# The first norm's shift and scale vectors: sixteen tiles with the weights as the stationary operand, instead of four on VectorE and twelve as rows

## The chip, the core and the metric

The kernel runs on one core of a Trainium2 chip. The metric is the device time of one execution in microseconds (us). TensorE is called PE in the profile, its weight loads PEld, VectorE DVE, ScalarE ACT, GpSimd POOL and the queue that issues the DMAs SP.

## The reference, cut to what matters

The program is two layers of a transformer-like trunk over 640 tokens (512 latent, 128 context) of width 1024. A layer normalises its input with a shift and a scale that come from a conditioning vector, projects it, runs three token mixers, merges them, and ends in a normalised MLP:

```python
mod = jax.nn.silu(cond) @ lp['w_mod'] + lp['b_mod']
sh1, sc1, gt1, sh2, sc2, gt2 = jnp.split(mod, 6, axis=-1)
h = rms_norm(x, lp['g_norm1']) * (1 + sc1) + sh1
... = jnp.split(h @ lp['w_in'], offsets, axis=-1)
```

There are two conditioning vectors, one for latent and one for context tokens. sh1 and sc1 of layer 0 are 2048 columns of w_mod, 8.4 MB in float32, and no projection can start without them. All the rest of w_mod (the other 80 tiles of 128 columns) is needed later.

## The kernel before, in words

Activations lie with channels on the partitions: x is eight tiles of 128 channels by 640 tokens, worked in two halves of 256 and 384 tokens. The large projections split each operand into a rounded part and a rest, so that each block takes three matmuls (L104 to L106, or the same three lines with operands exchanged); load_w loads a weight tile, rounds it on ACT (L97) and takes the rest on DVE or, in the first projections, on POOL (L99).

Nothing orders the work by hand. The program is written as one stream; a planner that is part of the framework puts each engine's instructions, and the issues on the SP queue, into an order by priority (program order) and by when it reckons them ready. On the chip each engine then works strictly in that order, and an instruction that waits holds up all behind it. SP also waits where a buffer has to be released.

Before the first projection (run, L1350 to L1375) the kernel does this:

- mod_first (three calls): 512 shift or scale columns at a time. The conditioning, two columns wide, is the stationary operand and the weights stream through, 512 columns per matmul (L223); float32 matmuls leave two records each. The two rows that come out are copied (L225), transposed (L228) and finished on DVE. Its weights come in 1 MB pieces into two buffers, mraw.
- cond_rows: 16 matmuls (L198) and four ACT copies spread the conditioning over all partitions, in condb.
- mod_tile (four calls at the start): the other 512 columns as dot products on DVE against condb (L209), weights in four 512 KB tiles, sraw.
- stat_add: squares of x on ACT (L262, L266), summed on DVE (L267). norm_scale: column sums by matmuls against a vector of ones (L285), the inverse root on DVE (L126 to L133, twelve small instructions for each half), and its spread over partitions by matmuls (L289).
- norm_apply: per channel tile and token part, nt (DVE, L300), hh (ACT, L303) and hl (DVE, L304).
- consts2 and tables load masks (two buffers, cast on DVE, L175), rope tables and a row; then mla_down starts three projections: proj_tail, and proj_nat twice. Its first two outputs (proj_tail, 48 matmul records 192 columns wide) come first, then proj_nat, 256 wide.

Later, at the start of layer 0's merge, cond_rows runs once more, and 80 further mod_tile calls are strewn over merge, out_proj and mlp, with one buffer, modw.

Of the kernel before, what the change touches and what calls it, by code (L numbers as in the profile page):

```python
# [11 lines left out]
F32 = mybir.dt.float32  # L12
# [4 lines left out]
ALU = mybir.AluOpType  # L17
# [4 lines left out]
D = 1024  # L22
# [46 lines left out]
    "xin": ("xin", 3), "mjunk": ("mj", 1), "condb": ("mj", 1), "modw": ("mj", 1), "mraw": ("st", 2), "sraw": ("st", 4), "maskf": ("st", 2), "mrow": ("st", 2), "uh": ("mlp", 8), "ul": ("mlp", 8), "relu": ("mlp", 3),  # L69
# [5 lines left out]
class Net:  # L75
# [125 lines left out]

    def mod_tile(self, l, i, buf="modw"):

        nc = self.nc
        w = self.S([128, 1024], F32, buf)
        nc.sync.dma_start(w, self.a["wmod"][l, i])
        for s in range(2):
            junk = self.S([128, 1024], mybir.dt.bfloat16, "mjunk")
            nc.vector.tensor_tensor_reduce(  # L209
                out=junk, in0=w, in1=self.condb[:, s], scale=1.0, scalar=0.0,  # L210
# [4 lines left out]
    def mod_first(self, b, kind):  # L215

        nc = self.nc
        p = self.P([128, 512], "g")
        for j in range(2):
            w = self.S([128, 4, 512], F32, "mraw")  # L220
            nc.sync.dma_start(w, self.a["wmods"][kind, b, j])
            for k in range(4):
                nc.tensor.matmul(p[0:2], self.csil[:, j * 4 + k::8], w[:, k], start=(j + k == 0), stop=(j + k == 4))  # L223
        row = self.S([2, 512], F32, "mrow")
        nc.scalar.copy(row, p[0:2])  # L225
        p = self.P([128, 4, 2], "g")
        for i in range(4):
            nc.tensor.transpose(p[:, i], row[:, i * 128:i * 128 + 128], self.ident[0:2, 0:2])  # L228
        i0 = kind * 8 + b * 4
        nc.vector.tensor_copy(self.modv[0][:, i0:i0 + 4], p)  # L230
        self.mod_fin(0, i0, 4)
# [26 lines left out]
    def stat_add(self, x, half):  # L258
# [8 lines left out]
        nc.vector.tensor_tensor(self.sq[:, c0:c1], self.sq[:, c0:c1], t[:, :c1 - c0], op=ALU.add)  # L267
# [1362 lines left out]
```

## Time and profile before

| what | value |
|---|---|
| median of three runs | 2676.58 us (2673.47 to 2679.17) |
| profiled execution, its own time | 2678.4 us |
| its span, first to last instruction | 2676.6 us |
| mean granted TensorE clock | 0.978 of full |
| TensorE matmul busy | 2538.1 us, 95% of the span |
| VectorE, ScalarE, GpSimd busy | 60%, 45%, 16% |

Busy time is the union of an engine's instructions; a pipelined matmul's record lasts longer than the step from one to the next, so rates are read from the start times. A clock of 1.00 is 2.4 GHz and 0.50 is 1.2 GHz. An arrow in square brackets says for how long the engine was idle before and what released it.

### The profile page before, as it was taken

The numbers are of one execution on the slowest core, as the hardware profiler recorded it, in microseconds if no ns is written. First come the engines' busy times: TensorE is split into PE (matmuls) and PEld (weight loads), VectorE is DVE, ScalarE is ACT, GpSimd is POOL, SyncE is SP. The second block draws the span as 40 slices with busy tenths as digits, with TensorE's granted clock in tenths as the row PEclk, the third lists the DMA queues.
The fourth block names the chain that finished last, engine by engine and source line by source line (L and its number), as shares of the span: only waits on it lengthen the run. The fifth ranks groups of instructions, "written<-read, shape, count | busy, mean of one in ns | idle before, by whom it ended". The sixth has DMA issues, their size and how long they took to land.

```text
span 2676.6 us, 45051 instructions
## 1 busy us (share of the span) xinstructions
PE 2538.1 (95%) x17596; PEld 2446.5 (91%) x17596; DVE 1596.4 (60%) x3635; ACT 1192.4 (45%) x2323; POOL 432.9 (16%) x582
## 2 busy tenths in 40 slices
PE   6999999799898999999989998998989999999999
PEld 3988899788898999999989888987879999999999
DVE  6488664676866776666365776647855346333332
ACT  4476775465222342232335776756642335132230
POOL 2021131310222021020121222213002101010110
PEclk8999999899999999999999999998999999999999
DMA  6111111312745444444221112122134242222221
GB/s 250 40 46 68 57 56 40 98 54 70 257 147 167 165 142 150 150 150 135 87 78 52 47 57 71 41 74 72 49 118 156 74 141 75 79 72 78 73 78 48
DMA packets 105268, 258.47 MB, mean 97 GB/s; under 512 B 11808, under 2 KB 43296, under 8 KB 104288
## 3 DMA queue, kind: packets, MB, share of 16 engines
q1 hardware_dynamic: 105056, 255.59, 28.5%
q8 instruction: 139, 2.28, 0.3%
q14 instruction: 73, 0.60, 0.1%
HBM read 229.43 MB, written 26.12 MB: 95 GB/s over the span
## 4 chain that ended last, share of the span: by engine, by line
PE 72%; DVE 12%; ACT 7%; DMA 4%; issue 3%; POOL 1%; SPq 0%; DVEq 0%; ACTq 0%; POOLq 0%
PE g L105 18%; PE g L104 18%; PE g L106 18%; DMA modw<-wmod 2%; PE f L104 2%; PE f L106 2%; PE f L105 2%; DVE mjunk L209 2%; PE go L498 2%; PE y L1018 1%; PE g L814 1%; DVE wlo L99 1%; PE g L1010 1%; DVE sm_m L746 1%; ACT whi L97 1%
## 5 line engine op out<-in xcount | busy, mean ns | idle before, releaser
L97 ACT CAST whi<-wraw 128x1024 fp32r<-128x1024 f32 (+2 forms) x236 | 220.1, 932 | 440.2 <-PE g L105 373.8
L99 DVE TENSOR_TENSOR wlo<-wraw,whi 128x1024 fp32r<-128x1024 f32 (+3 forms) x230 | 258.9, 1127 | 225.7 <-ACT whi L97 220.0
L106 PE MATMUL g<-hh,wlo 128*128 128x256 f32 (+1 forms) x1072 | 332.2, 310 | 4.2 <-DVE wlo L99 4.2
L104 PE MATMUL g<-hh,whi 128*128 128x256 f32 (+1 forms) x1072 | 332.0, 310 | 3.2 <-ACT gth L1179 2.7
L105 PE MATMUL g<-hl,whi 128*128 128x256 f32 (+1 forms) x1072 | 331.6, 309 | 0.0
L1292 POOL TENSOR_TENSOR relu<-relu 128x256 f32<-128x256 f32 (+1 forms) x128 | 110.6, 865 | 805.2 <-ACT uh L1291 795.3
L209 DVE CUSTOM_DVE_ANT_0 mjunk<-modw,condb 128x1024 bf16<-128x1024 f32 x160 | 199.5, 1247 | 68.5 <-DMA modw<-wmod 65.6
L97 ACT CAST xhi<-xraw 128x1024 fp32r<-128x1024 f32 (+1 forms) x80 | 83.7, 1046 | 283.6 <-PE g L105 264.2
L106 PEld LDWEIGHTS g<-hh,wlo 128*128 128x128 f32 x1072 | 203.2, 190 | 5.4 <-DVE wlo L99 5.4
L104 PEld LDWEIGHTS g<-hh,whi 128*128 128x128 f32 x1072 | 202.9, 189 | 4.8 <-ACT gth L1179 3.3
L105 PEld LDWEIGHTS g<-hl,whi 128*128 128x128 f32 x1072 | 203.3, 190 | 0.0
L1241 DVE SCALAR_TENSOR_TENSOR x<-g,moda,x 128x256 f32<-128x256 f32 (+1 forms) x192 | 78.4, 435 | 200.6 <-PE g L106 200.6
L104 PE MATMUL g<-hh,xhi 128*128 128x384 f32 (+1 forms) x544 | 168.1, 309 | 0.0
L106 PE MATMUL g<-hh,xlo 128*128 128x384 f32 (+1 forms) x544 | 168.0, 309 | 0.0
L105 PE MATMUL g<-hl,xhi 128*128 128x384 f32 (+1 forms) x544 | 167.8, 308 | 0.0
L104 PE MATMUL g<-uh,xhi 128*128 128x384 f32 (+1 forms) x512 | 158.2, 309 | 0.0
L106 PE MATMUL g<-uh,xlo 128*128 128x384 f32 (+1 forms) x512 | 158.0, 309 | 0.0
L105 PE MATMUL g<-ul,xhi 128*128 128x384 f32 (+1 forms) x512 | 158.0, 309 | 0.0
L106 PE MATMUL g<-uh,wlo 128*128 128x384 f32 (+1 forms) x512 | 158.0, 309 | 0.0
L105 PE MATMUL g<-ul,whi 128*128 128x384 f32 (+1 forms) x512 | 157.9, 308 | 0.0
L104 PE MATMUL g<-uh,whi 128*128 128x384 f32 (+1 forms) x512 | 157.9, 308 | 0.0
L1228 POOL TENSOR_TENSOR x<-x,th 128x256 f32<-128x256 f32 x64 | 75.7, 1188 | 496.8 <-DVE th L1226 496.6
(445 smaller groups left out, 7664.1 us busy)
## 6 DMA issues: line engine op xcount, KB each, us to landing
modw<-wmod SPq DMA_DIRECT2D x80, 512.0 KB, 3.5
wraw<-w SPq DMA_DIRECT2D x64, 512.0 KB, 3.5
xraw<-w SPq DMA_DIRECT2D x64, 512.0 KB, 3.5
wraw<-wfm SPq DMA_DIRECT2D x62, 512.0 KB, 3.5
wraw<-wn SPq DMA_DIRECT2D x36, 512.0 KB, 3.6
wraw<-wo SPq DMA_DIRECT2D x48, 256.0 KB, 3.2
yin<-yd SPq DMA_DIRECT2D x24, 320.0 KB, 3.9
mraw<-wmods SPq DMA_DIRECT2D x6, 1024.0 KB, 6.1
```

Source lines behind the costliest of these rows:

```text
L97: nc.scalar.copy(hi, raw)
L99: eng.tensor_tensor(lo, raw, hi.bitcast(F32), op=ALU.subtract)
L104: mm(out, wh, xh, start=first, stop=False)
L105: mm(out, wh, xl, start=False, stop=False)
L106: mm(out, wl, xh, start=False, stop=last)
L209: nc.vector.tensor_tensor_reduce(out=junk, in0=w, in1=self.condb[:, s], scale=1.0, scalar=0.0, op0=ALU.mult, op1=ALU.add, accum_out=self.m ...
L498: nc.tensor.matmul(p[:, hd], km[:, hd, cs], qm[:, hd, cs])
L746: nc.vector.tensor_reduce(out=nm, in_=sc, axis=ax, op=ALU.max, negate=True)
L814: nc.tensor.transpose(p[:, i * 256 + j * 128:i * 256 + j * 128 + 128], pts[j][:, (k0 + i) * 128:(k0 + i) * 128 + 128], self.ident)
L1228: nc.gpsimd.tensor_tensor(mg[m][:, c0:c1], mg[m][:, c0:c1], t[:, c0:c1], op=ALU.add)
L1241: self.nc.vector.scalar_tensor_tensor(dst[:, p0:p1], p[:, p0 - c0:p1 - c0], self.moda[l][:, kind * 8 + m, s:s + 1], src[:, p0 - o:p1 - o], ...
L1292: nc.gpsimd.tensor_tensor(r[:, :n], r[:, :n], r[:, :n], op=ALU.mult)
```

## The change

The sixteen tiles of 128 columns (eight of shift, eight of scale) are all computed by PE with the roles exchanged: the weight block of 128 by 128 is the stationary operand, the two columns of conditioning stream through, eight matmuls a tile. The result lies on the partitions already, so that one ACT instruction per tile adds the bias (and, for the scale, multiplies by the gain) and no row is copied or transposed. Weight tiles of 512 KB use twelve buffers: two are loaded ahead of x, ten behind it, four as buffers come free. The order is scale and shift of channel tile 0, then of tile 1, and so on, with norm_apply following tile by tile. The inverse norm is computed once for all five blocks of 128 tokens. The sum of squares of the second half goes to POOL. The first cond_rows call and the four mod_tile calls are gone; the remaining cond_rows, at the merge, loads the two conditioning rows by a DMA that broadcasts them to all partitions and applies the silu there, with half of it left to the dot product's scale. The weights' host layout changes with it.

```diff
     "xin": ("xin", 3), "mjunk": ("mj", 1), "condb": ("mj", 1), "modw": ("mj", 1), 
-    "mraw": ("st", 2), "sraw": ("st", 4), "maskf": ("st", 2), "mrow": ("st", 2), ...
+    "mraw": ("st", 12), "maskf": ("st", 2), ...
     def cond_rows(self):
         cb = self.S([128, 2, 1024], F32, "condb")
+        nc.sync.dma_start(cb, self.a["condr"].to_broadcast([128, 2, 1024]))
         for s in range(2):
-            for q in range(2):
-                p = self.P([128, 512], "g")
-                for j in range(4):
-                    c = self.csil[:, s * 8 + q * 4 + j:][:, 0:1]
-                    nc.tensor.matmul(p[:, j * 128:j * 128 + 128], c.to_broadcast([128, 128]), self.ident)
-                nc.scalar.copy(cb[:, s, q * 512:q * 512 + 512], p)
+            th = self.S([128, 1024], F32, "modw")
+            nc.scalar.activation(th, cb[:, s], AF.Tanh, scale=0.5)
+            nc.vector.scalar_tensor_tensor(cb[:, s], th, 1.0, cb[:, s], op0=ALU.add, op1=ALU.mult)
...
-    def mod_first(self, b, kind):
+    def mod_load(self, j):
+        w = self.S([128, 8, 128], F32, "mraw")
+        self.nc.sync.dma_start(w, self.a["wmods"][j])
+        return w
+    def mod_first(self, k, kind, w):
         p = self.P([128, 512], "g")
-        for j in range(2):
-            w = self.S([128, 4, 512], F32, "mraw")
-            nc.sync.dma_start(w, self.a["wmods"][kind, b, j])
-            for k in range(4):
-                nc.tensor.matmul(p[0:2], self.csil[:, j * 4 + k::8], w[:, k], start=(j + k == 0), stop=(j + k == 4))
-        row = self.S([2, 512], F32, "mrow")
-        nc.scalar.copy(row, p[0:2])
...
+        for j in range(8):
+            nc.tensor.matmul(p[:, 0:2], w[:, j], self.csil[:, j::8], start=(j == 0), stop=(j == 7))
+        i = kind * 8 + k
+        if kind == 0:
+            nc.scalar.activation(self.moda[0][:, i], p[:, 0:2], AF.Identity, bias=self.bmod[:, 0, i:i + 1])
+        else:
+            nc.scalar.activation(
+                self.moda[0][:, i], p[:, 0:2], AF.Identity, bias=self.bg[:, k:k + 1], scale=self.vec[:, 0, k:k + 1])
...
-        nc.vector.tensor_tensor(self.sq[:, c0:c1], self.sq[:, c0:c1], t[:, :c1 - c0], op=ALU.add)
+        (eng or nc.vector).tensor_tensor(self.sq[:, c0:c1], self.sq[:, c0:c1], t[:, :c1 - c0], op=ALU.add)
...
+    def norm_scale_all(self):
+        bc = [self.P([128, 512], "n") for half in range(2)]
+        st = bc[0][:, 384:389]
+        for i in range(5):
+            nc.tensor.matmul(st[:, i:i + 1], self.sq[:, i * 128:i * 128 + 128], self.one)
+        r = self.S([128, 5], F32, "nr5")
+        self.rsqrt(r, st, 1.0 / D, 5)
+        for i in range(5):
+            half, j = (0, i) if i < 2 else (1, i - 2)
+            nc.tensor.matmul(bc[half][:, j * 128:j * 128 + 128], r[:, i:i + 1].to_broadcast([128, 128]), self.ident)
...
-            self.mod_first(0, 1)
+            order = [(k, kind) for k in range(8) for kind in (1, 0)]
+            ws = {j: self.mod_load(j) for j in range(2)}
             for k in range(8):
                 nc.sync.dma_start(xs[k], a["x"][:, k])
                 for i in range(2):
-                    self.stat_add(xs[k], i)
-            self.cond_rows()
-            for i in range(4):
-                self.mod_tile(0, i, "sraw")
+                    self.stat_add(xs[k], i, nc.gpsimd if i else nc.vector)
             self.norm_begin()
-            for half in range(2):
-                self.norm_scale(half)
-            self.mod_first(1, 1)
-            self.mod_first(1, 0)
-            for k in (0, 4):
-                for half in range(2):
-                    self.norm_apply(0, 0, xs, half, range(k, k + 4))
+            for j in range(2, 12):
+                ws[j] = self.mod_load(j)
+            for j in range(2):
+                self.mod_first(*order[j], ws.pop(j))
+            self.norm_scale_all()
+            for k in range(8):
+                for j in (2 * k, 2 * k + 1):
+                    if j > 1:
+                        self.mod_first(*order[j], ws.pop(j))
+                    if j + 10 < 16 and j + 10 > 11:
+                        ws[j + 10] = self.mod_load(j + 10)
+                self.norm_apply(0, 0, xs, 0, (k,))
+                if k < 6:
+                    self.norm_apply(0, 0, xs, 1, (k,))
+            self.norm_apply(0, 0, xs, 1, (6, 7))
             self.consts2()
```

## Rows read from the trace of the kernel before

**Rows 1.** The page, part 1: busy us (share of the span) and instructions of each engine

```profile
PE 2538.1 (95%) x17596; PEld 2446.5 (91%) x17596; DVE 1596.4 (60%) x3635; ACT 1192.4 (45%) x2323; POOL 432.9 (16%) x582
```

**Rows 2.** Windows of 10 us: PE, PEld, DVE, ACT, POOL busy; clock, DMA share, GB/s

```profile
10.00:20.00 10.00, 9.33 (x42) 4.07 (x41) 6.12 (x16) 7.58 (x19) 0.00 (x0) 1.00 1.04 417
...
60.00:70.00 10.00, 10.00 (x65) 10.00 (x65) 6.82 (x19) 4.33 (x12) 4.67 (x13) 0.73 0.17 57
...
100.00:110.00 10.00, 10.00 (x75) 10.00 (x75) 6.81 (x39) 5.10 (x19) 0.00 (x0) 1.00 0.13 37
```

**Rows 3.** Timeline of the start: start us, us, engine, line, operation, tiles, forms

```profile
7.80 8.51 PE L223 MATMUL g<-mraw,csil 128*2 128x512 f32 x16 [7.80 <-DMA mraw<-wmods]
...
20.99 1.17 PE L285 MATMUL n<-one,sqacc 128*128 128x1 f32 x10
...
21.68 0.15 DVE L126 TENSOR_SCALAR rq_v<-n 128x2 f32<-128x2 f32 x1
...
32.12 2.50 PE L289 MATMUL n<-ident,nr 128*128 128x128 f32 x10 [5.05 <-DVE nr L133]
...
52.97 0.36 PE L104 MATMUL g<-whi,hh 128*128 128x192 f32 x1
...
57.85 0.53 PE L106 MATMUL g<-xhi,hl 128*128 128x192 f32 x1 [1.49 <-DVE hl L304]
...
65.27 0.40 PE L104 MATMUL g<-whi,hh 128*128 128x256 f32 x1
```

**Rows 4.** Timeline of the SP queue at the start

```profile
2.58 0.91 SPq L221 DMA_DIRECT2D mraw<-wmods  x2
...
19.02 0.33 SPq L311 DMA_DIRECT2D rowb<-row  x1
32.53 0.80 SPq L174 DMA_DIRECT2D maskf<-mask  x2
...
46.18 0.33 SPq L174 DMA_DIRECT2D maskf<-mask  x1
```

**Rows 5.** Short windows with the granted clock (last three columns as in Rows 2)

```profile
38.00:38.50 0.50, 0.50 (x3) 0.09 (x2) 0.31 (x1) 0.50 (x3) 0.50 (x1) 0.87 0.00 0
...
60.00:64.00 4.00, 4.00 (x21) 4.00 (x20) 4.00 (x8) 2.25 (x5) 2.37 (x1) 0.50 0.03 12
...
65.00:65.50 0.50, 0.50 (x4) 0.50 (x4) 0.50 (x3) 0.50 (x2) 0.00 (x0) 0.56 0.98 401
...
1382.00:1386.00 4.00, 3.09 (x13) 2.85 (x13) 2.10 (x12) 0.00 (x0) 0.00 (x0) 0.50 0.38 131
```

**Rows 6.** Timeline of PE at layer 1's first norm

```profile
1382.36 1.44 PE L285 MATMUL n<-one,sqacc 128*128 128x1 f32 x6 [6.37 <-DVE sqacc L267]
1383.66 0.51 PE L106 MATMUL g<-whi,hl 128*128 128x192 f32 x1
...
1389.75 0.31 PE L105 MATMUL g<-wlo,hh 128*128 128x192 f32 x1
```

**Rows 7.** Groups by form (DVE in 0:75, POOL in all): count, busy us, mean ns

```profile
L304 DVE SCALAR_TENSOR_TENSOR hl<-nt,moda,hh 128x256 fp32r<-128x256 f32 x16 | 11.9, 757 | 0.9 <-ACT hh L303 0.8
L209 DVE CUSTOM_DVE_ANT_0 mjunk<-sraw,condb 128x1024 bf16<-128x1024 f32 x8 | 9.8, 1223 | 0.1
L300 DVE SCALAR_TENSOR_TENSOR nt<-n,moda,x 128x256 f32<-128x256 f32 x16 | 7.2, 472 | 0.5 <-PE n L289 0.5
...
L1292 POOL TENSOR_TENSOR relu<-relu 128x384 f32<-128x384 f32 x64 | 63.4, 991 | 268.8 <-ACT uh L1291 266.1 <-DVE ul L1293 2.7
...
L1228 POOL TENSOR_TENSOR x<-x,th 128x384 f32<-128x384 f32 x32 | 45.3, 1416 | 47.4 <-DVE th L1226 47.1 <-DMA th<-gd 0.3
```

**Rows 8.** Timeline of the merge's start, layer 0

```profile
601.35 0.33 SPq L206 DMA_DIRECT2D modw<-wmod  x1
...
665.44 3.74 PE L198 MATMUL g<-ident,csil 128*128 128x128 f32 x32
...
672.83 0.98 PE L104 MATMUL g<-yh,whi 128*128 128x256 f32 x3 [3.66 <-ACT yh L137]
```

More of the change, by code (lines that the diff above doesn't have):

```diff
@@ L68 @@
     "yin": ("mrg", 2), "yh": ("mrg", 4), "oyh": ("mrb", 4), "oyl": ("mrb", 4), "yl": ("mrg", 4), "th": ("mrg", 2), "mh": ("mo", 8), "ml": ("mo", 8),
-    "xin": ("xin", 3), "mjunk": ("mj", 1), "condb": ("mj", 1), "modw": ("mj", 1), "mraw": ("st", 2), "sraw": ("st", 4), "maskf": ("st", 2), "mrow": ("st", 2), "uh": ("mlp", 8), "ul": ("mlp", 8), "relu": ("mlp", 3),
+    "xin": ("xin", 3), "mjunk": ("mj", 1), "condb": ("mj", 1), "modw": ("mj", 1), "mraw": ("st", 12), "maskf": ("st", 2), "uh": ("mlp", 8), "ul": ("mlp", 8), "relu": ("mlp", 3),
 }
@@ L192, in cond_rows, with mod_tile @@
         cb = self.S([128, 2, 1024], F32, "condb")
+        nc.sync.dma_start(cb, self.a["condr"].to_broadcast([128, 2, 1024]))
         for s in range(2):
-            for q in range(2):
-                p = self.P([128, 512], "g")
-                for j in range(4):
-                    c = self.csil[:, s * 8 + q * 4 + j:][:, 0:1]
-                    nc.tensor.matmul(p[:, j * 128:j * 128 + 128], c.to_broadcast([128, 128]), self.ident)
-                nc.scalar.copy(cb[:, s, q * 512:q * 512 + 512], p)
+            th = self.S([128, 1024], F32, "modw")
+            nc.scalar.activation(th, cb[:, s], AF.Tanh, scale=0.5)
+            nc.vector.scalar_tensor_tensor(cb[:, s], th, 1.0, cb[:, s], op0=ALU.add, op1=ALU.mult)
         self.condb = cb
-    def mod_tile(self, l, i, buf="modw"):
+    def mod_tile(self, l, i):
         nc = self.nc
-        w = self.S([128, 1024], F32, buf)
+        w = self.S([128, 1024], F32, "modw")
         nc.sync.dma_start(w, self.a["wmod"][l, i])
@@ L209, in mod_tile @@
             nc.vector.tensor_tensor_reduce(
-                out=junk, in0=w, in1=self.condb[:, s], scale=1.0, scalar=0.0,
+                out=junk, in0=w, in1=self.condb[:, s], scale=0.5, scalar=0.0,
                 op0=ALU.mult, op1=ALU.add, accum_out=self.modv[l][:, i, s:s + 1])
@@ L256, in stat_begin, with stat_add @@
         self.sq_first = {0: True, 1: True}
-    def stat_add(self, x, half):
+    def stat_add(self, x, half, eng=None):
         nc = self.nc
@@ L1538, in _layout @@
     d["wmod"] = np.ascontiguousarray(g["w_mod"].transpose(0, 2, 1).reshape(DEPTH, 48, 128, 1024))
-    wm = g["w_mod"][0, :, 0:2048].reshape(2, 4, 128, 2, 2, 512)
-    d["wmods"] = np.ascontiguousarray(wm.transpose(3, 4, 0, 2, 1, 5))
+    d["condr"] = cond.reshape(1, 2, 1024)
+    wm = g["w_mod"][0, :, 0:2048].reshape(8, 128, 2, 8, 128)[:, :, ::-1]
+    d["wmods"] = np.ascontiguousarray(wm.transpose(3, 2, 1, 0, 4).reshape(16, 128, 8, 128))
     d["bmod"] = np.ascontiguousarray(g["b_mod"].reshape(DEPTH, 48, 128).transpose(2, 0, 1))
```

13 lines of the change are left out of this document (6 added, 7 removed).

## The prediction

> **What bounds the kernel now.** I read the page's busy shares first: PE is busy for 95% of the span [rows 1], so a stage before PE's steady work is worth what it moves the start of that work. Then the windows and the timeline of the first 110 us. PE runs 512-column mod_first matmuls from 7.80, and DMA moves 417 GB/s from 10 to 20 us [rows 2, 3]. The column sums end at 22.2 (20.99 and 1.17), but the inverse root starts at 21.68 and its spread over partitions (L289) only at 32.12 [rows 3]: DVE puts eight dot products of 1.22 us (L209, 9.8 us) between the small root instructions [rows 7]. Then two mod_first calls hold PE and the norm; the first projection matmul comes at 52.97, and after twelve of them and two more PE waits for hl until 57.85 [rows 3]. From there PE has no gap: it is busy for 10.00 of 10 us in each of the five windows from 60 to 110 us [rows 2]. So the landmark is the first 256-column matmul of proj_nat, at 65.27, when proj_tail's first 48 records are done (12 at 52.97, two at 55.6, 34 from 57.85). A shift of that landmark reaches the end.
>
> The clock belongs to the reading. From 57.85 PE works gap-free on 192-column matmuls at half clock [rows 3, 5]: 34 records in 7.42 us, 0.217 us each, and the clock rises only at 65.4 (0.56 on average from 65.0 to 65.5).
>
> **The change, part by part.**
>
> *Removed.* The L209 group (9.8 us of DVE), 48 mod_first records, the transposes, and cond_rows' 32 records (3.74 us in the later call) [rows 3, 7, 8]. The root's twelve instructions close up from 10.4 us (21.68 to 32.12) to about 1.6 us (twelve of 0.15 us, partly overlapped, by the length of L126) [rows 3].
>
> *Added on PE.* Sixteen tiles of eight float32 matmuls, two records each: 256 records with a 128 by 128 stationary block and two columns. The nearest row has the same form with one column, L285. At full clock it takes 1.17 us for 10, 0.117 each [rows 3]. At half clock it takes 1.30 us for 6 (1382.36 to the next matmul at 1383.66), 0.217 each, in a window whose clock is 0.50 [rows 5, 6]. So the tile costs 1.87 us or 3.47 us, and all sixteen 30 or 56 us. Before, the streamed form took 8.51 us for a quarter of the columns, the transposes aside [rows 3], and DVE did another quarter. The weight load, not the two columns, sets the price.
>
> The Trainium skill (TensorE: Matmul & The Clock Gate, section LDWEIGHTS) has a load's time as its columns over 1.2, about 107 ns for 128, without a word of the clock. By that, as an estimate, a tile would be 1.7 us at either clock. The row at half clock (0.217) disagrees, so the sum below does not use it.
>
> *Which clock.* Of gap-free streams, 512-column ones had the clock back by 38.0 to 38.5, after starting at 34.6 behind L289 (32.12 and 2.50) [rows 3, 5]. The 192-column ones needed 7.5 us at 57.85 and 6.1 us at 1383.66 (first faster step at 1389.75) [rows 3, 6]. Being busy is therefore not all; a stream with fewer columns was slower to bring the clock back although it had no gap. Two columns lie far beyond the 192, on the slow side, and before tile 0 PE has done nothing. I take half clock throughout: 0.217, and keep 0.117 as the other end.
>
> *The order of events at half clock.* In the run before, 1 MB issued at 2.58 releases PE at 7.80 [rows 3, 4]. Half as much ahead lands 1.3 us earlier at the 417 GB/s of [rows 2], so tile 0 runs from 6.5 and tile 1 ends at 13.4. Then x (2.62 MB) and tile 2 land: 3.7 MB more than tile 0, 8.8 us by the same rate, 15.3. PE has from there 14 tiles (224 records, 48.6 us), the column sums (10 records, 2.2) and the spread (2.5, as L289 at half clock [rows 3]): 53.3 us, end 68.6. The planner reckons by its own durations, and its order may leave PE waiting up to 2 us for the root: 69 is my value, 68.6 to 71 the bounds.
>
> *What hides beside it.* DMA: 16 tiles and x are 11 MB, 27 us at that rate, done about 33; the twelve buffers take the SP wait for mod_first's release away. rowb (19.02) and the masks, with the rope table, are moved behind five more megabytes at most, about 35 us, and the POOL tables with them; they are needed after 100 us. DVE's norm_apply is six instructions a channel tile of 0.47 to 0.76 us for the 256-wide ones [rows 7], about 2.6 us a tile against 6.9 us of PE. POOL's seven 384-wide sums cost between 0.99 and 1.42 us each [rows 7]; 7 to 10 us from the second x tile at about 10.3, so the sums are complete by 17 to 20, while PE still has tiles 2 and 3. If that cover were gone (full clock) it would be a few us. The sixteen small ACT instructions, about 0.2 us each, hold what is queued behind them on ACT: the rounding of the first projection weights. If those come behind the last tile, PE waits 2.7 us (cast and POOL rest) or more. SP still has a mask load that waits for a cast on DVE: at 32.53 and 46.18 [rows 4] such loads stood ahead of projection weights, and with DVE paced by PE the third one can come near 65 us. Zero to 5 us for these two, and I take none, since proj_tail's 48 records cover the next weights.
>
> *After the tiles.* 48 records of proj_tail: PE restarts at half clock and by the two 192-column rows keeps it for about 6.9 us, 32 records, then 16 at the 0.117 that a weight load took at full clock [rows 3]: 8.8 us. Landmark 69 + 8.8 = 77.8 instead of 65.27: **+12.5 us**.
>
> *At the merge.* Before, PE ends L198 at 669.2 and then waits 3.66 us for yh until 672.83 [rows 8], so 3.74 us less on PE gains nothing there. In its place: 1 MB of broadcast DMA (2.5 us at 417 GB/s), two tanh and two DVE passes of 1024 columns (1.2 us each, as L209's size). If SP issues it where the first modw load stood, at 601.35 [rows 8], it is hidden under the mixer; if only after 665, it delays yin and DVE's first dot products by up to 5 us. No reason excludes either; I take 1 us. The factor 0.5 in the dot product and the other mod_tile calls cost nothing, being one operand of an instruction that is there anyhow.
>
> *Sum.* 12.5 + 1 = 13.5 us on the profiled execution's 2678.4 us (span 2676.6, 1.8 us around it) gives 2691.9. That execution lies 1.8 us above the median of the three runs, so against the median the forecast is **2690 us**.
>
> **Rivals.**
>
> *Half clock, as above, with or without small stalls* (chance 0.78). Bounds: 68.6 start and no merge cost, +12; 71, 5 us of queue stalls and 5 at the merge, +24; an earlier clock rise or a few overlapped records, down to +8. So 2685 to 2700.
>
> *The tiles run at full clock* (0.14), the rival on the other side. PE from 15.3: 224 records of 0.117, 26.2 us, sums and spread 2.4 us, end 44; DVE's eight channel tiles from about 24 end at 45 too. Then 48 records of 0.117, 5.6 us: landmark 50.6, 14.7 us earlier; with the merge's 1 us, 2663 us against the median. For it: PE would be busy without a gap from 15 us on. Against it: the 192-column rows above. It decides from about 0.17 us a record, halfway between the two prices: below that the change is a gain. The Trainium skill (the same page, section The HAM clock gate) says that the clock is held back by default and that activity of PE releases it; by that rule, taken simply, this rival would be the outcome. The gap-free 7.5 us at half clock from 57.85 disagree with it in that form.
>
> *The clock changes on the way, or stalls elsewhere hide the rest* (0.08). At about 0.17 us a record, 291 records end where they do now, and the time stays at 2677, plus or minus 5. Nothing in the rows speaks for it but that the price lies between two ends.
>
> **Numbers.** Under 0.2%, 5.4 us, a measurement of this kernel can hardly be told from no change. Slower by more: 0.78. Same: 0.07, most of the third case. Faster: 0.15, the full clock and a part of the third. The likeliest case's own range is 2685 to 2700. To leave out no more than 2 in 10 it has to take in part of the middle case: 2677 to 2701.
>
> **What would show it.** Right: L223's new form at 0.21 to 0.22 us a record with a granted clock of 0.50 from about 6 to 69 us; the root in under 3 us; no DVE dot products before 100 us; the landmark near 78 us, and from there on both traces alike but shifted. Wrong: a clock of 1.00 in the windows from 20 to 45 us and the landmark near 50 (the second case); tiles waiting for DMA or SP rather than PE (a stall that I priced at nothing); or a merge whose first matmul comes more than 5 us later than the shift.

## The result, and the profile after

The change makes the kernel slower: 2714.74 us (median of four runs, 2710.32 to 2717.15) beside 2677.56 us for the kernel before, measured with it, a ratio of 1.0139 [1.0121, 1.0157]. The forecast was 2690 (2677 to 2701). The direction was right, and so was the main cause; the size was not. The profiled execution spans 2715.4 us, 38.8 more than before. All ratios here are taken over fast runs alone, which for one of the runs below (streamed columns mixed in) are two of four, so a median can lie beside its ratio.

The timeline of PE in the run after (start, length, instruction, count; in brackets the idle time ahead and what ended it):

```profile
6.47 6.96 PE L223 MATMUL g<-csil,mraw 128*128 128x2 f32 x32 [6.47 <-DMA mraw<-wmods]
24.70 1.01 PE L295 MATMUL n<-one,sqacc 128*128 128x1 f32 x4 [11.27 <-DVE sqacc L265]
26.04 1.44 PE L295 MATMUL n<-one,sqacc 128*128 128x1 f32 x6 [0.33 <-POOL sqacc L265]
27.34 6.97 PE L223 MATMUL g<-csil,mraw 128*128 128x2 f32 x32
34.17 2.48 PE L300 MATMUL n<-ident,nr 128*128 128x128 f32 x10
36.44 40.96 PE L223 MATMUL g<-csil,mraw 128*128 128x2 f32 x192
81.49 0.74 PE L104 MATMUL g<-whi,hh 128*128 128x192 f32 x2 [4.09 <-ACT whi L97]
83.38 0.53 PE L105 MATMUL g<-wlo,hh 128*128 128x192 f32 x1 [1.14 <-POOL wlo L99]
...
89.04 0.36 PE L105 MATMUL g<-wlo,hh 128*128 128x192 f32 x1
89.24 0.28 PE L106 MATMUL g<-whi,hl 128*128 128x192 f32 x1
...
91.36 0.30 PE L104 MATMUL g<-whi,hh 128*128 128x256 f32 x1
```

These answer to [rows 3]. The landmark is, as in the prediction, the first 256-column matmul of proj_nat. A record of the new form takes 40.96 / 192 = 0.213 us from the first to the last of twelve tiles, which is the half-clock price of L285 in [rows 6]. Three waits are new. PE stands still for 11.3 us between tile 1 and the column sums, which the planner put ahead of tile 2. After the last tile, which ends at 77.4, it waits 4.1 us for a cast on ACT and 1.1 us for POOL's rest. The 192-column records of proj_tail then go at half pace until 89.1, and the landmark is at 91.36 instead of 65.27.

ACT's timeline shows what both waits hang on:

```profile
10.05 0.35 ACT L228 ACTIVATE moda<-g,bg,vec 128x2 f32<-128x2 f32 x1 [5.90 <-PE g L223]
13.46 0.26 ACT L226 ACTIVATE moda<-g,bmod 128x2 f32<-128x2 f32 x1 [3.06 <-PE g L223]
13.62 0.82 ACT L260 ACTIVATE sqacc<-x 128x256 f32<-128x256 f32 x2
...
17.89 0.83 ACT L264 ACTIVATE sqt<-x 128x384 f32<-128x384 f32 x2 [0.80 <-POOL sqacc L265]
...
80.51 0.20 ACT L333 ACTIVATE lams<-lams 128x2 f32<-128x2 f32 x1 [1.44 <-DVE lams L332]
80.62 0.81 ACT L97 CAST whi<-wraw 128x768 fp32r<-128x768 f32 x1
```

The finishing instructions of tiles 0 and 1 stand ahead of the first square, which so starts at 13.62 (10.92 before). Each pair of squares then waits for POOL's sum, 1.62 us a channel tile. At the other end the first cast stands behind the last hh and behind an exponential that waits for DVE.

What the shift of 38.8 us is made of, from the starts of four instructions and the ends of the two traces (latq, df_yn and yh are tiles of the mixers and of the merge; the last column is rounded for itself):

| stretch | before | after | growth |
|---|---|---|---|
| start to the landmark | 65.27 | 91.36 | 26.1 |
| landmark to the first latq matmul | 61.8 | 66.3 | 4.5 |
| latq to the first df_yn weight load (end of the mixers) | 461.6 | 461.4 | -0.2 |
| df_yn to the first yh weight load (merge) | 84.2 | 86.6 | 2.5 |
| yh to the end of the span | 2003.8 | 2009.7 | 5.9 |

### The profile page after: what moved, and what is told of

The parts are those of the page before. It is cut to its first block, busy times and chain, and to the rows that moved or that the text cites. A ratio compares the mean times of both kernels' runs of the same rounds, so it can differ in the third digit from the quotient of the medians.

```text
span 2715.4 us, 45313 instructions
## 1 busy us (share of the span) xinstructions
PE 2564.0 (94%) x17728; PEld 2496.8 (92%) x17728; DVE 1580.2 (58%) x3594; ACT 1191.3 (44%) x2330; POOL 433.0 (16%) x589
## 4 chain that ended last, share of the span: by engine, by line
PE 70%; DVE 11%; ACT 7%; DMA 5%; issue 3%; POOL 2%; SPq 0%; DVEq 0%; ACTq 0%; POOLq 0%
PE g L104 17%; PE g L105 17%; PE g L106 17%; DMA modw<-wmod 3%; PE g L223 2%; PE f L104 2%; DVE mjunk L207 2%; PE go L510 2%; PE f L106 2%; PE f L105 2%; PE y L1030 1%; PE g L826 1%; DVE wlo L99 1%; DVE sm_m L758 1%; ACT whi L97 1%
## 5 line engine op out<-in xcount | busy, mean ns | idle before, releaser
L207 DVE CUSTOM_DVE_ANT_0 mjunk<-modw,condb 128x1024 bf16<-128x1024 f32 x160 | 198.0, 1238 | 81.2 <-DMA modw<-wmod 80.7
L97 ACT CAST xhi<-xraw 128x1024 fp32r<-128x1024 f32 (+1 forms) x80 | 83.4, 1042 | 287.4 <-PE g L105 261.0
```

Of the source, the lines that this page charges most:

```text
L97: nc.scalar.copy(hi, raw)
L207: nc.vector.tensor_tensor_reduce(out=junk, in0=w, in1=self.condb[:, s], scale=0.5, scalar=0.0, op0=ALU.mult, op1=ALU.add, accum_out=self.m ...
```

## The experiments

Each was timed beside runs of the kernel before on the same chip (median 2681 to 2683 there), so the ratios are what is compared; that of the changed kernel is 1.0139. The expectations reckon from the 2677.56 us of the result, so a ratio times that base is what is held against their times. A shift of a few us shows more clearly at the landmark of a trace than in such a ratio.

### Which price, and which clock

**Extra matmuls ahead of the tiles.**

```diff
+        p = self.P([128, 512], "n")
+        for i in range(n): nc.tensor.matmul(p, self.dw, self.dx, ...)   # zeros, bf16, 512 columns
...
+            self.warm(14)          # ahead of tile 0
...
+            self.warm(50)          # ahead of norm_scale_all
```

> The changed kernel with 64 extra matmuls on zeros (bf16, 512 columns, results unused), 14 put ahead of tile 0 and 50 in the wait for the column sums, where PE was idle from 13.4 to 24.7 us. Theory A (0.217 is the low clock's price, and two-column matmuls keep a clock that is once raised): from about 13 us on a tile's records step by 0.117; tiles 2 to 15 take 26 us instead of 49, the landmark comes 20 to 24 us earlier, 2691 to 2695. Theory B (it is the low clock's price, but a stream of two-column matmuls lets the clock fall again): 0.117 at first, then 0.217 for the rest; 2700 to 2712, and the profile shows the place. Rival C (0.217 is what this form costs in a long row, at any clock): steps of 0.217 throughout, 2713 to 2717.

1.0115 [1.0098, 1.0132]. PE's timeline, then two windows (length, busy time of PE, PEld, DVE, ACT and POOL, granted clock, DMA share, GB/s):

```profile
7.61 1.84 PE L235 MATMUL g<-csil,mraw 128*128 128x2 f32 x16
...
12.09 9.22 PE L223 MATMUL n<-dx,dw 128*128 128x512 bf16 x42
23.59 0.98 PE L307 MATMUL n<-one,sqacc 128*128 128x1 f32 x4 [2.28 <-DVE sqacc L277]
...
26.15 6.97 PE L235 MATMUL g<-csil,mraw 128*128 128x2 f32 x32
...
35.25 40.96 PE L235 MATMUL g<-csil,mraw 128*128 128x2 f32 x192
```

```profile
12.00:21.00 9.00, 9.00 (x45) 4.10 (x44) 4.49 (x6) 5.43 (x14) 4.43 (x5) 1.00 1.03 412
...
34.00:64.00 30.00, 30.00 (x143) 30.00 (x142) 13.01 (x34) 8.89 (x25) 4.09 (x18) 0.50 0.23 70
```

Tiles 0 and 1, amid the extra matmuls, took 1.84 us for 16 records, 0.115 each. Then PE idled 2.28 us before the sums, the clock fell to 0.50, and the twelve last tiles took 40.96 us as in the changed kernel, 0.213 a record. The two prices are those of the clock, so rival C falls; whether the gap or the form lost the clock stayed open.

**The same without the gap.** The second call is `self.warm(66)`.

> The changed kernel with 80 extra matmuls on zeros (bf16, 512 columns, results unused), 14 put ahead of tile 0 and 66 ahead of the column sums: as the run with 64 of them, but without the gap of 2.3 us before the column sums, in which that run's granted clock fell from 1.00 to 0.50 at about 22 us. Theory A (it was the gap that lost the clock; two-column matmuls in a row keep what they are given): tiles 2 to 15 step by 0.115 to 0.117, 26 us instead of 49; landmark near 66 to 70 instead of 91.4, and 2689 to 2694. Theory B (a row of two-column matmuls lets the clock fall by itself, gap or not): the granted clock falls to 0.50 some microseconds after the sums, at around 28 to 36 us, and stays there; landmark 84 to 89, 2708 to 2713.

1.0091 [1.0076, 1.0106]. Windows, and PE's timeline in two of its stretches (the counts are of the stretch asked for):

```profile
26.00:28.00 2.00, 2.00 (x20) 2.00 (x19) 1.19 (x8) 0.00 (x0) 0.00 (x0) 1.00 1.03 410
28.00:29.00 1.00, 1.00 (x8) 1.00 (x8) 0.81 (x5) 0.35 (x1) 0.00 (x0) 0.69 0.92 365
29.00:40.00 11.00, 11.00 (x52) 11.00 (x53) 0.48 (x1) 0.88 (x4) 0.00 (x0) 0.50 0.80 230
40.00:60.00 20.00, 20.00 (x96) 20.00 (x95) 7.88 (x21) 5.33 (x15) 3.93 (x18) 0.50 0.09 36
60.00:74.00 14.00, 14.00 (x67) 14.00 (x67) 6.40 (x17) 4.08 (x12) 0.00 (x0) 0.50 0.01 2
```

```profile
26.39 2.17 PE L235 MATMUL g<-csil,mraw 128*128 128x2 f32 x18
...
45.71 24.46 PE L235 MATMUL g<-csil,mraw 128*128 128x2 f32 x114
```

Eighteen records took 2.17 us at a clock of 1.00. Then, with PE busy throughout, the clock fell (0.69 on average from 28 to 29 us) to 0.50, and it stayed there until the tiles were done. So theory B holds: a row of two-column matmuls lost a clock that it had been given, without a gap. A kept clock would have saved about 22 us, as an estimate (224 records at 0.115 instead of 0.213); the landmark, at 88.68, is 2.7 us earlier. The landmark lies in theory B's range; the time lies between the two, 6 us below B's.

**Streamed columns mixed in.**

```diff
             nc.tensor.matmul(p[:, 0:2], w[:, j], self.csil[:, j::8], ...)
+            if j % 4 == 3:
+                nc.tensor.matmul(q[0:2], self.csil[:, j::8], w[:, j - 3:j + 1], start=True, stop=True)
```

> The changed kernel with two more matmuls in each tile, four records of 512 streaming columns against two stationary ones (results unused), one behind each four of the tile's eight. At the low clock a tile would cost 3.5 + 4 x 0.43 = 5.2 us, at full clock 1.9 + 4 x 0.22 = 2.8 us. Theory A/B (columns streamed bring the clock back, and 0.217 is the low clock's price): after a few tiles steps of 0.117, tiles 2 to 15 in 39 to 50 us, not slower than the changed kernel although PE does half as much again: 2700 to 2716. Rival C (0.217 is the form's own price): the added 56 matmuls in tiles 2 to 15 just add to it, 12 us at full clock and 24 at the low one: 2726 to 2740.

1.0107 [1.0087, 1.0127]. PE's timeline:

```profile
10.01 1.87 PE L223 MATMUL g<-csil,mraw 128*128 128x2 f32 x8
...
19.00 1.87 PE L225 MATMUL g<-mraw,csil 128*2 128x512 f32 x2
...
32.68 2.48 PE L302 MATMUL n<-ident,nr 128*128 128x128 f32 x10
...
38.20 1.05 PE L223 MATMUL g<-csil,mraw 128*128 128x2 f32 x8
39.18 1.02 PE L225 MATMUL g<-mraw,csil 128*2 128x512 f32 x2
```

Eight records take 1.87 us in the first tiles and 1.05 from 35 us on, after the spread of the norm, and so on to 86 us: 50 us in which the same two-column records, with a streamed matmul between, keep the fast pace. But the mix did not bring that pace about: from 6.45 to 20.9 us PE did the same mix without a gap at the first price, and the step came behind the spread's ten 128-column matmuls (32.68). A streamed record took about 0.9 us at that price and 0.5 later, twice what had been expected. PE does more work than in the changed kernel, and yet the time is not told from it (the intervals overlap).

**The roles exchanged back.**

```diff
-            nc.tensor.matmul(p[:, 0:2], w[:, j], self.csil[:, j::8], ...)
+            nc.tensor.matmul(p[0:2, 0:128], self.csil[:, j::8], w[:, j], ...)
+        row = self.S([2, 128], F32, "mrow")
+        nc.scalar.copy(row, p[0:2, 0:128])
+        p = self.P([128, 512], "g")
+        nc.tensor.transpose(p[:, 0:2], row, self.ident[0:2, 0:2])
```

> The changed kernel with only the operands of the 16 tiles exchanged back: two columns of conditioning are the stationary operand, 128 weight columns stream; ACT copies the 2 by 128 row, PE transposes it, and the same ACT instruction finishes it. Theory (the 128-column weight load sets 0.217 us a record at the low clock): a record now costs 0.11 to 0.14 us at the same pace, a tile 1.8 to 2.2 us plus up to 1 us for the copy and the transpose; tiles 2 to 15 take about 42 us instead of 49 and the landmark comes near 80 to 84, 2703 to 2708. Rival (at the low clock every fp32 matmul costs 0.217 whatever is loaded): tiles cost 3.5 us plus 1 us, landmark near 105, 2725 to 2730.

1.0027 [1.0015, 1.0039]: some 30 us of the loss are gone, more than either theory gave. PE's timeline and three windows:

```profile
6.46 3.57 PE L223 MATMUL g<-mraw,csil 128*2 128x128 f32 x16 [6.46 <-DMA mraw<-wmods]
...
29.10 1.91 PE L223 MATMUL g<-mraw,csil 128*2 128x128 f32 x16
31.36 0.22 PE L227 MATMUL g<-ident,mrow 2*128 2x2 f32 x1 [0.34 <-ACT mrow L225]
...
62.82 0.36 PE L104 MATMUL g<-whi,hh 128*128 128x192 f32 x1
...
68.79 0.30 PE L104 MATMUL g<-whi,hh 128*128 128x256 f32 x1
```

```profile
18.00:26.00 8.00, 5.36 (x23) 4.06 (x24) 3.40 (x14) 1.35 (x3) 2.09 (x3) 0.50 1.03 410
...
27.00:28.00 1.00, 1.00 (x8) 0.81 (x8) 0.33 (x2) 0.51 (x1) 0.00 (x0) 0.79 1.03 410
28.00:60.00 32.00, 26.44 (x221) 18.10 (x219) 18.29 (x45) 17.52 (x49) 10.14 (x22) 1.00 0.45 145
```

The theory failed in its reason. A record with 128 streaming columns against two stationary ones costs 3.57 / 16 = 0.223 us at the low clock and 0.119 at the high one, the same as the form of the change. What differs is the clock, for which no run shows a reason: this form fell to 0.50 in the wait for the sums as well, but had it back at 27.5 and kept it through 32 us in which PE was busy only 83% of the time. Of the 22.6 us at the landmark, the sums come 4.6 us earlier (they end at 22.8; ACT's squares no longer stand behind the tiles' finish), tiles 2 to 15 with the spread take 10.0 us less (40 instead of 50, with 14 transposes in them), the wait behind the last tile (6.0) is gone, and 48 projection records take 6.0 us at full clock instead of 8.0.

### The waits around the tiles

**Both halves' sums on DVE.**

```diff
-                    self.stat_add(xs[k], i, nc.gpsimd if i else nc.vector)
+                    self.stat_add(xs[k], i)
```

> The changed kernel with the sums of squares of both halves on DVE again (POOL does none). In the changed kernel POOL's 0.99 us for each of seven sums paces ACT's squares at 1.62 us a channel tile, and the column sums end at 27.3. Theory (POOL sets the pace): with DVE a channel tile takes 0.9 to 1.1 us from 13.6 on, the squares are summed by about 22, the landmark (first 256-wide proj_nat matmul, 91.36) comes 2 to 4 us earlier, about 88, and the end with it, near 2711. Rival (x arrives at that pace anyway, or ACT is the limit): sums end at 26 to 27.5, landmark within 1 us of 91.4.

One run, 2709.2 us, span 2707.4. PE's timeline:

```profile
21.74 1.01 PE L295 MATMUL n<-one,sqacc 128*128 128x1 f32 x4 [8.45 <-DVE sqacc L265]
22.61 3.55 PE L223 MATMUL g<-csil,mraw 128*128 128x2 f32 x16
```

The sums start at 21.74 instead of 24.70 and the planner puts tile 2 between them; the landmark comes at 87.69, 3.7 us earlier. POOL set that pace. The end moved by 8.0, more than the cause can give; what that is comes below.

**Five mask buffers.**

```diff
-    "maskf": ("st", 2)
+    "maskf": ("st", 5)
```

> The changed kernel with five mask buffers instead of two, so that no mask load on SP waits for a cast on DVE, which stands behind all of norm_apply. Theory (queue stall): in the changed kernel SP is blocked from 37.3 to 79.9 us, and the second projection weights are issued only from 80.7. With the masks out of the way they are issued before 40 us. The first cast (80.6) does not move, since its weights are there already and it waits for hh and lams on ACT; the landmark (first 256-wide proj_nat matmul, 91.36) stays within 1 us, but the stalls behind it (0.35 at 93.45, 2.04 at 101.58) shrink: 2 to 5 us off, about 2711. Rival: the raw weight buffers (two and one) hold these loads back anyhow; then nothing moves, 2714 to 2716.

1.0125 [1.0110, 1.0140], which leaves both theories open; the trace shows the rival. SP now issues the second projection weights at 39.5 instead of 80.7, but the loads behind them wait for the raw buffers, which come free only behind the casts and POOL's rests (83.9 to 102.8). From the landmark (92.34) to latq it is 66.6 us, as in the changed kernel (66.3): the wait only changed its name.

**Masks, tables and lambda ahead of the tiles**, on top of that:

```diff
             self.norm_scale_all()
+            self.consts2()
+            self.tables(0)
```

> The changed kernel with five mask buffers, and with the masks, the rope tables and the small lambda computation placed in the program ahead of the tile loop instead of behind it. In the changed kernel the first weight cast on ACT (80.62) stands behind a lambda exponential that waits for DVE, and this behind the last hh (77.6). Theory (that queue order costs the 5 us between the last tile, 77.4, and the first stretch of projections, 83.4, and the loads held back behind it cost 4.5 us more until the first latq matmul): the first cast runs at 76 to 78, the landmark comes 3 to 5 us earlier than 91.36 and the first latq matmul 6 to 9 us earlier than 157.6; 2705 to 2709. Rival (the casts still wait for the last tiles, and the raw buffers for the casts): landmark 90 to 92, latq 156 to 158, 2713 to 2716.

1.0119 [1.0104, 1.0135], not told from the changed kernel by its time; span 2708.4. The first cast runs at 78.84 instead of 80.62, the landmark comes at 88.76 (2.6 earlier) and the first latq matmul at 155.3 (2.3 earlier). The wait between the last tile and the steady projections falls from 6.0 to 4.1 us (77.55 to 81.60). The rest, and the slow stretch until latq, stay: the casts still come with the last tiles, and the raw buffers behind them. The theory had 6 to 9 us until latq, so it priced that order at more than twice its worth.

### The merge

**The part alone, in the kernel before.**

```diff
+        nc.sync.dma_start(cb, self.a["condr"].to_broadcast([128, 2, 1024]))
+        for s in range(2):
+            th = self.S([128, 1024], F32, "modw")
+            nc.scalar.activation(th, cb[:, s], AF.Tanh, scale=0.5)
+            nc.vector.scalar_tensor_tensor(cb[:, s], th, 1.0, cb[:, s], op0=ALU.add, op1=ALU.mult)
```

> The kernel before with one part of the change alone: at layer 0's merge the conditioning rows come by the broadcasting DMA with tanh and a DVE pass, in place of 16 matmuls and four copies; the first cond_rows call and all else stay. Theory (the merge part costs by itself): in the changed kernel the shift against the run before grows from 30.5 us at 589 to 32.9 us at the first yh matmul and to 36.1 us at the first uh tile. If that is this part, its first 256-wide proj_nat matmul stays at 65.3, the merge's first yh matmul comes 2 to 4 us after 672.8, and the time is 2680 to 2684. Rival (the growth comes from the order that the planner gives the rest, or from loads that are late since the start): 2675 to 2679, with the yh matmul at 672 to 674.

1.0014 [1.0005, 1.0022], 3.8 us: the landmark is at 65.38, the yh load 2.7 us late, the span 6.2 longer. The rows are ready so early that the first dot product starts at 629.1 instead of 668.0, and PE gets a wait that the kernel before hasn't. PE's waits from 580 to 1040 us (waiting, waited for: total us, times, longest):

```profile
PE g L106 <- DVE wlo L99: 9.1, 5, 3.5
PE g L104 <- ACT yh L137: 7.8, 2, 7.3
PE n L296 <- DVE sqacc L278: 6.6, 1, 6.6
PE g L1158 <- DVE df_yn L1153: 3.2, 1, 3.2
```

The dot products of 1.2 us stand in DVE's queue amid the last mixer's df_yn chain. The changed kernel has the same row, 3.2 us.

**The part undone, in the changed kernel.**

```diff
-        nc.sync.dma_start(cb, self.a["condr"].to_broadcast([128, 2, 1024]))
...
+                for j in range(4):
+                    c = self.csil[:, s * 8 + q * 4 + j:][:, 0:1]
+                    nc.tensor.matmul(p[:, j * 128:j * 128 + 128], c.to_broadcast([128, 128]), self.ident)
+                nc.scalar.copy(cb[:, s, q * 512:q * 512 + 512], p)
```

> The changed kernel with one part undone: the merge's conditioning rows come by 16 matmuls and four copies again, without the broadcasting DMA, tanh and DVE pass. Theory (that part costs 4 to 6 us by itself, as it did when it was put alone into the kernel before: yh 2.7 us late, uh 5.7, end 6.2): landmark at 91.4 as in the changed kernel, shift at the first yh matmul 30 us instead of 32.9, end 4 to 6 us earlier, 2708 to 2711. Rival (the growth of the shift in the merge comes from the late start, and the part is hidden there): 2713 to 2716.

1.0122 [1.0109, 1.0136]: not told from the changed kernel. The stretch from df_yn to yh shrank from 86.6 to 85.4 us, but the landmark came 0.5 later and the rest scattered. Over all 17 profiled kernels the stretch is cleaner than the times: 86.3 to 87.3 us in the nine with the new rows, 83.5 to 85.4 in the eight with the old ones. So the part costs about 2.5 us there, and my 4 to 6 for it was too much.

### What is left of the change

**Roles, sums and merge put back** (the edits of three runs above together, `mod_first`, `stat_add` and `cond_rows`).

```diff
+            nc.tensor.matmul(p[0:2, 0:128], self.csil[:, j::8], w[:, j], ...)
+                    self.stat_add(xs[k], i)
+                nc.scalar.copy(cb[:, s, q * 512:q * 512 + 512], p)
```

> The changed kernel with three things put back: the operands' roles (two conditioning columns stationary, 128 weight columns streaming), both sums of squares on DVE, and the merge's conditioning rows by matmuls. What is left of the change: all 16 tiles on PE in its order, twelve buffers, one root. Theory (three separate causes that add up: clock 26 us, POOL's sums 2 to 4, merge 4 to 6): landmark at 65 to 67 instead of 91.36, and 2678 to 2684, within 0.3% of the kernel before. Rival (they overlap, and the late queue of casts and weight loads remains): landmark near 69 as with the roles alone, 2685 to 2690.

1.0016 [1.0007, 1.0026], in the theory's range by the time, but by its landmark (69.86) it is the rival. The sums end at 21.8, 5.5 us earlier than in the changed kernel. But casts that the planner put amid the row copies held PE's transposes for 1.0 to 2.0 us three times, the clock reads 0.50 from 60 us on, and the 48 records of proj_tail took 7.6 us instead of the 6.0 of the run with the roles alone.

**The same, with the masks and tables ahead of the tiles as well.**

```diff
+    "maskf": ("st", 5)
             self.norm_scale_all()
+            self.consts2()
+            self.tables(0)
```

> The changed kernel with everything taken out that the runs so far named: operands' roles exchanged back (streaming weights), both sums of squares on DVE, the merge's rows by matmuls, five mask buffers, masks and tables ahead of the tile loop. What is left of the change: all 16 tiles on PE in pieces of 128 columns, twelve buffers, one root. Theory (these were the causes, and the rest of the change is about neutral): landmark 64 to 68, the segment from the landmark to the first latq matmul 61 to 63 us, 2675 to 2682. Rival (something else in the change costs as well): 2685 to 2690, as with the roles alone.

1.0013 [1.0002, 1.0024], landmark 66.65, and 61.8 us from there to latq, as before. So with clock, sums, queue order and merge taken out, about 3.5 us of the 37 are left (0.5 to 6.4 by the interval), of which the landmark shows 1.4. So these were the causes; what each is worth is read from the traces, for the exchange of roles moves the clock, the sums and the last casts at once.

### The streamed form for all sixteen, to see what could be gained

**The kernel before, with a fourth mod_first call** in place of cond_rows and the four mod_tile calls:

```diff
-            self.cond_rows()
-            for i in range(4):
-                self.mod_tile(0, i, "sraw")
             self.norm_begin()
+            self.mod_first(0, 0)
```

> The kernel before with its own streamed form for all four quarters of the shift and scale columns (two-column stationary conditioning, 512 weight columns per matmul): the four dot-product tiles on DVE and the first spreading of the conditioning rows are gone, a fourth mod_first call takes their place, and the raw weights have five 1 MB buffers; the norm's two roots and the merge are as before. Theory (streamed columns raise the clock and DVE is free for the root): the root takes under 4 us instead of 10.4, the last mod_first ends at 36 to 42 instead of about 50, norm_apply follows by 50; landmark at 52 to 56 instead of 65.27, 2664 to 2668. Rival (the late casts and masks of the changed kernel come with this order as well): landmark 60 to 66, 2672 to 2678. Other rival (the streamed form at the low clock throughout, 8.5 us a call): last call ends at 46 to 50, no gain.

1.0001 [0.9991, 1.0011]: no gain, and the theory fails. The landmark gained 2.1 us. The second call ran at 0.50 (9.87 us), and norm_apply, which can't finish before the last call, kept DVE busy past 60.

**With 34 extra matmuls in PE's pauses.**

```diff
+            self.warm(14)
             self.mod_first(0, 1)
+            self.warm(20)
```

> The run with the fourth mod_first call (512 streaming columns, all four quarters on PE) with 34 extra matmuls on zeros (bf16, 512 columns, results unused), 14 ahead of the first call and 20 behind it, where PE is idle. Without them its first call took 8.73 us, its second 9.87 at a granted clock of 0.50 from 22 to 28 us, its fourth ended at 49.7, and norm_apply kept DVE busy to 60 (landmark 63.2). Theory (the clock is up from the first call, and each takes 7 us): the fourth call ends at 43 to 45, DVE's last four channel tiles by 54 to 55, landmark 55 to 57, 8 to 10 us before the kernel before's, and 2668 to 2673. Rival (a gain at the start is given back at the merge, as the 2 to 3 us of that run were): 2675 to 2680.

**In pieces of 256 columns, with these too.**

```diff
-            w = self.S([128, 4, 512], F32, "mraw")
+            w = self.S([128, 4, 256], F32, "mraw")
...
+            for k in range(0, 8, 2):
+                if k > 1:
+                    self.mod_first(k // 2, 1)
+                    self.mod_first(k // 2, 0)
+                for half in range(2):
+                    self.norm_apply(0, 0, xs, half, range(k, k + 2))
```

> The run before it in this call in pieces of 256 columns: eight mod_first calls in the order of the channel tiles, ten raw buffers of 512 KB, norm_apply two channel tiles at a time, and the same 34 extra matmuls. Theory (norm_apply follows the calls, so that only two channel tiles are left behind the last call): last call ends at 45 to 49, DVE by 51 to 55, landmark 52 to 56, 2666 to 2672. Rival (the waits for copy and transposes, 0.7 us a call, eat it, or the clock is lost in the pauses): landmark 58 to 63, 2673 to 2679.

**Without pauses:** 48 extra matmuls, and a call's transposes and finish (mod_end) behind the next call's matmuls.

```diff
+                    if 1 < j < 8:
+                        r2 = self.mod_first(*todo[j])
+                    if j > 1:
+                        self.mod_end(*todo[j - 1], r)
+                        r = r2
```

> The run with eight mod_first calls of 256 streaming columns and 34 extra matmuls on zeros, now with 48 of them (14, 10 and 24) and with each call's transposes behind the next call's matmuls. There PE was idle for 2.82 us ahead of the sums, ran the second call in 5.30 instead of 3.62 us, and waited 0.5 us for ACT in each call; the last call ended at 51.0 and the landmark came at 60.55. Theory (these pauses are what is left): last call ends at 45 to 47, landmark 54 to 58, 2667 to 2673. Rival (DVE's norm_apply, 2.6 us a channel tile, or the weights' casts are the limit by now): landmark 59 to 61, 2674 to 2679.

0.9989 [0.9980, 0.9997], 0.9993 [0.9984, 1.0001] and 0.9992 [0.9983, 1.0001]; landmarks 64.90, 60.55 and 57.51. None of the three reached its theory's time. The first is a gain of 3 us, 0.11%, and the only one whose interval leaves out no change. That can be chance among so many runs: its trace shows no source for it, for its second call ran at 0.50 until 30 us again (9.97 us in all) and its yh came 2.2 us later than in the kernel before. It is less than the 0.2% of the prediction's bound.

The last has what I asked for: a granted clock of 1.00 from 14 to 45 us and the last call done at 45.7. Its landmark is 7.8 us ahead of the kernel before's, latq 4.7, yh 5.4, and the end of the profiled execution 0.6 behind. By the ratio 2 us reach the end, 4.6 at most. PE in that run:

```profile
47.33 0.47 PE L104 MATMUL g<-whi,hh 128*128 128x192 f32 x2 [0.54 <-ACT whi L97]
49.22 0.53 PE L105 MATMUL g<-wlo,hh 128*128 128x192 f32 x1 [1.43 <-POOL wlo L99]
...
60.82 0.38 PE L105 MATMUL g<-xlo,hh 128*128 128x256 f32 x1 [1.59 <-POOL xlo L99]
```

PE waits for a cast and for POOL's rest, the clock falls to 0.50 from 49 to 55.7, so that 46 records of proj_tail take 8.3 us, and behind the landmark two waits for xlo cost 2.6. DVE and POOL there:

```profile
51.48 4.94 POOL L99 TENSOR_TENSOR wlo<-wraw,whi 128x1024 fp32r<-128x1024 f32 x2
```

```profile
54.11 2.59 DVE L320 SCALAR_TENSOR_TENSOR hl<-nt,moda,hh 128x256 fp32r<-128x256 f32 x1
```

While POOL subtracts for the weights' rests, a hl of 0.48 us takes up to 2.6. PE shows no wait for a hl in this run, so that is not what held it.

The rest is scatter of the executions, and not of the plan. From yh to the end the eight kernels with the old rows have the same instructions in the same order on every engine (by tiles and forms), and so have the nine with the new ones; yet they take 2002.3 to 2009.8 and 2001.4 to 2009.7 us there (2003.8 before, 2009.7 after). What differs among them, as far as the traces show, is how long the granted clock reads 0.50 in that stretch: 61.4 us in the execution of 2002.3, 77.8 in that of 2009.8, 64.9 before and 84.5 after (correlation with the time over the 17 executions 0.80). Why it differs, no run shows. The kernel before's own runs lay between 2673.2 and 2689.1 us beside one group of experiments.

## Why the prediction was right, and where it was wrong

The forecast had the mechanism and missed the size: it added 13.5 us, and the two traces differ by 38.8. The steps that failed are the order of the queues around the tiles, which it put at 2 us at most ahead of them and at nothing behind them (8.4 and 6.0 us), the late casts, which it had not (4.5 us), and the merge (1.5 us more). The last 5.9 us lie within the scatter of executions.

**Right: the price and the clock.** The sum took 0.217 us a record and it was 0.213 to 0.218 in all fourteen late tiles; the root took 2.4 us (27.52 to 29.9), under the 3 that were to show it, though not the 1.6 reckoned; DVE has no dot products at the start. That a row of two-column matmuls would not bring the clock back is shown more strongly than the prediction said it: with the clock given, the row lost it. The rule weighed there (the Trainium skill, TensorE: Matmul & The Clock Gate, section The HAM clock gate: activity of PE releases the clock) does not hold in that simple form: in the run without the gap PE was busy from 26 to 74 us and sat at 0.50 from 29 on.

**Right in effect, its reason not shown: "The weight load, not the two columns, sets the price".** With the operands exchanged the load is two columns wide and 128 stream, and a record costs the same at either clock (0.223 and 0.119). So a smaller load alone is worth nothing here; the two forms differ in what they do to the clock.

**Wrong: "its order may leave PE waiting up to 2 us for the root", 68.6 to 71 for the end of the tiles.** They ended at 77.4, 8.4 us behind the forecast's 69: PE stood idle for 11.3 us ahead of the sums instead of the 1.9 from 13.4 to 15.3. I had the sums complete by 17 to 20 with tiles 2 and 3 as cover. The planner put the sums ahead of tile 2 in PE's order, so there was no cover, and they came at 24.7 to 27.3, for ACT's squares stood behind the finish of tile 1 and went at POOL's 1.62 us a channel tile. The exchange of sums shows 3.7 us of this; with roles and sums both exchanged the sums end 5.5 us earlier. The order of queues was the term to bound: I had priced POOL's sums, but not what it meant to be behind a tile on ACT.

**Wrong: the queue stalls behind the last tile, "zero to 5 us, and I take none".** They were 6.0 us (77.4 to 83.4), of which the run with the tables first shows 1.9 to be queue order. The cover I named, 48 records of proj_tail, hides later weights; the wait was for the first. Two of the 48 records ran within that wait; the other 46 took 8.0, where 8.8 had been forecast for all. Together with the forecast's 12.5 and the sums' 8.4 this is the landmark's shift: 12.5 + 8.4 + 6.0 - 0.8 = 26.1.

**Missing: what the late casts do after the landmark.** 4.5 us until latq: two waits for xlo, 2.4 us in all, and a granted clock of 0.83 from 100 to 110 us. "From there on both traces alike but shifted" does not hold for the first 60 us.

**Mis-sized: the merge, 1 us.** It is about 2.5 to yh. I had looked for a late DMA; in fact the rows came early, and the dot products went in ahead of df_yn.

**Not a term at all: the scatter of executions.** 5.9 us from yh to the end lie within what executions of the same order show there. The clock reads 0.50 for 19.6 us longer in that stretch of the run after. Whether the late start has a part in it stays open; no run separates it.

**The rival on the other side** (full clock, 2663) was too good by its own steps. The run without pauses has its clock and ends its tiles at 46, yet its landmark is 57.5 and not 50.6, and by the ratio 2 us of that reached the end. It is another form, with 48 extra matmuls, so it bounds the rival and does not test it.

## What to carry to other kernels

Read the clock beside the form: here a small matrix product with two streaming columns held PE at half clock for 41 us, and the same product with 128 streaming columns kept the full clock for 32. So put the long dimension on the streaming side; mixed in, streamed work kept a clock that was there, but did not bring one back in the first 14 us. When a step becomes PE's own, follow its finish on the other engines' queues: what stands behind a PE-paced instruction there (squares, casts) is what PE will wait for next. And executions of one and the same order differ by up to 8 us at their end here, so a forecast of 0.2% needs that scatter in its range, and a change of a few us is read at a landmark and over many runs, not at the end of one trace.

## What the runs showed of the hardware that was not expected

The clock column reads 1.00 from the start to the first recorded change: in the run after it says so until 100 us, while records step at the half-clock pace of 0.213. Two of its windows (columns as above):

```profile
60.00:70.00 10.00, 10.00 (x48) 10.00 (x49) 3.43 (x9) 2.85 (x8) 0.00 (x0) 1.00 0.01 2
...
100.00:110.00 10.00, 8.41 (x59) 8.42 (x60) 0.00 (x0) 3.64 (x14) 2.63 (x7) 0.83 0.16 52
```

Steps, not the column, tell the clock of such a stretch. With the roles exchanged, too, tile 0 steps by 0.223 and tile 1 (10.87 us) by 0.119, and the column reads 1.00 for both.

Two-column float32 matmuls with 128 by 128 stationary blocks let the clock fall from 1.00 to 0.50 in a row without a gap (the ten matmuls of the norm's spread stand in its middle), and kept it there to the row's end, 46 us later; a row with a 512-column matmul behind each four of them kept the fast pace for 50 us.

DVE's hl took 2.59 us instead of 0.48 beside POOL's subtraction: it starts at 54.11 and ends at 56.70, just behind POOL's two, which end at 56.42. The Trainium skill (SBUF — State Buffer, section SBUF: two separate sides) says that a DVE instruction with two inputs in SBUF and a GpSimd instruction that reads SBUF need one shared pair of ports, which the one that starts first holds for its whole length; these rows agree. The kernel before had it too, at 55.6, a hl of 2.20 us, and there PE waited for it, the 1.49 us until 57.85 in [rows 3].
